# SwiGLU on one core: four rows per partition stored as one 64 KiB piece, the second pair multiplied in quarters

## The chip, the core and the metric

The kernel runs on one core of a Trainium2 chip. VectorE (DVE) multiplies, ScalarE (ACT) applies the activation, and 16 DMA engines move data between the device's memory (HBM) and the core's 128-partition on-chip memory (SBUF). DMAs are issued from three places, each with its own queue on all 16 engines: SyncE (SP, queue q1 in the profile), ACT (q10) and GpSimd (POOL, q0). The time is device microseconds for one launch; lower is better. The time before is the median of three runs.

## The reference

```python
x = np.random.randn(8192, 8192).astype(np.float32)

def reference(x):
    a, b = np.split(x, 2, axis=-1)
    silu_b = b / (1 + np.exp(-b))
    return a * silu_b
```

Each row of 8192 float32 holds 4096 values of `a`, then 4096 of `b`; the output row is 4096 wide. The input is 268.4 MB and the output 134.2 MB, and each byte is moved once.

## The kernel before

**Tiling.** Two neighbouring rows belong to one partition, so a tile is 128 partitions x 2 rows: 64 KiB of input per partition (8 MiB in all), one contiguous block of HBM, and 32 KiB of output per partition (4 MiB), contiguous too. There are 32 tiles. Three slots of 64 KiB per partition (`slots`, L39) hold them in turn; tile `i` uses slot `i % 3`.

**One tile.** `load(i)` (L54, the DMA at L55) is issued from SP. `swiglu(i)` (L67) writes silu(b) over b on ACT (`gate`, L72) and then a times that on DVE (`prod`, L76), into the front 32 KiB of the same slot. `store(i)` (L81, the DMA at L85) sends that front to HBM. A page line with L72 is thus a gate, L76 a product, L55 a load and L85 a store.

**Order.** The order is written out by hand. Each engine runs its own instructions in program order, and an instruction waits for what `follows_from_others` (L44) leaves in place: a gate for its load, a product for its gate, a store for its product, and the load of tile `i + 3` for the store of tile `i`, whose slot it takes. SP issues the loads in order, so a load that waits holds back every later one. Once a DMA is issued its packets stand in that issuer's queue on the 16 DMA engines.

**Queues.** Stores go out from ACT, except for five of the odd tiles in the second half (17 to 25), which go out from POOL (L83), and the last tiles', which go out from SP.

**Head and tail.** Tile 0 is gated and multiplied one row at a time and its store split in three (512 KB, 1536 KB, 2048 KB), so that the second half of its slot can be reloaded early (L94 to L99, `free`); tiles 1 and 2 are done one row at a time with one store. The last tile is loaded in two halves (L115, L116); its second row is gated, and multiplied, in two pieces of 2048 columns, and each row is stored by itself (L118 to L121).

Of the kernel before, what the change touches and what calls it, by code (L numbers as in the profile page):

```python
# [1 line left out]

# [4 lines left out]

_SILU = mybir.ActivationFunctionType.Silu


@with_exitstack
def kernel(
    ctx: ExitStack,
    tc: tile.TileContext,
    x: bass.AP,
    out: bass.AP,
):

    nc = tc.nc
    N, M = x.shape
    half = M // 2
    P = nc.NUM_PARTITIONS
    R = 2
    BUFS = 3  # L30

    xv = x.tensor.reshape([N // R, R * M]).ap()
    ov = out.tensor.reshape([N // R, R * half]).ap()
    ntiles = N // (P * R)
    last = ntiles - 1

    pool = ctx.enter_context(tc.tile_pool(name="sbuf", bufs=1))
    ctx.enter_context(tc.manual_schedule())
    slots = [pool.tile([P, R * M], x.dtype, name=f"slot{s}") for s in range(BUFS)]  # L39
    loads, gates, prods, stores = ([[] for _ in range(ntiles)] for _ in range(4))  # L40

    newest = {}

    def follows_from_others(inst, i, current, earlier):  # L44


        targets = [t for kind in current for t in kind[i]]
        targets += [t for kind in earlier for j in range(i % BUFS, i, BUFS) for t in kind[j]]
        for t in targets:
            if t is not newest.get(inst.ins.engine):  # L50
                tc.declare_no_dep(inst.ins, t.ins, reason="ordered by the other waits")
        newest[inst.ins.engine] = inst

    def load(i, c0=0, cw=R * M, free=None):  # L54
        inst = nc.sync.dma_start(  # L55
            out=slots[i % BUFS][:, c0 : c0 + cw], in_=xv[i * P : (i + 1) * P, c0 : c0 + cw]
        )
        if free:
            for t in loads[i - BUFS] + gates[i - BUFS] + prods[i - BUFS] + stores[i - BUFS]:
                if t is not free and t is not newest.get(inst.ins.engine):  # L60
                    tc.declare_no_dep(inst.ins, t.ins, reason="ordered by the other waits")
            newest[inst.ins.engine] = inst
        else:
            follows_from_others(inst, i, [], [loads, gates, prods])
        loads[i].append(inst)

    def swiglu(i, k0=0, k1=R, c0=0, cw=half, gated=None):  # L67
        rows = slots[i % BUFS].rearrange("p (k s c) -> p k s c", k=R, s=2)
        a = rows[:, k0:k1, 0, c0 : c0 + cw]
        b = rows[:, k0:k1, 1, c0 : c0 + cw]  # L70
        o = slots[i % BUFS][:, : R * half].rearrange("p (k c) -> p k c", k=R)
        gate = nc.scalar.activation(out=b, in_=b, func=_SILU)  # L72
        follows_from_others(gate, i, [], [loads, gates, prods, stores])
        if gated:
            gated()
        prod = nc.vector.tensor_mul(out=o[:, k0:k1, c0 : c0 + cw], in0=a, in1=b)  # L76
        follows_from_others(prod, i, [loads], [loads, gates, prods, stores])
        gates[i].append(gate)
        prods[i].append(prod)

    def store(i, c0=0, cw=R * half):  # L81
        eng = nc.scalar if i < last - 1 else nc.sync
        if i % 2 and ntiles // 2 <= i < ntiles // 2 + 10:  # L83
            eng = nc.gpsimd
        inst = eng.dma_start(  # L85
            out=ov[i * P : (i + 1) * P, c0 : c0 + cw], in_=slots[i % BUFS][:, c0 : c0 + cw]
        )
        follows_from_others(inst, i, [loads, gates], [loads, gates, prods, stores])
        stores[i].append(inst)

    for i in range(BUFS):
        load(i)
    for i in range(last):
        if i == 0:  # L94

            swiglu(i, 0, 1)
            swiglu(i, 1, 2, gated=lambda: [store(0, 0, half // 4), store(0, half // 4, half * 3 // 4)])
            load(BUFS, M, M, free=prods[0][-1])
            store(i, half, half)  # L99
        elif i < BUFS:  # L100
            for k in range(R):
                swiglu(i, k, k + 1)
            store(i)
        else:
            swiglu(i)
            if i == last - 1:
                swiglu(last, 0, 1)
            store(i)
        nxt = i + BUFS
        if nxt == BUFS:  # L110
            load(nxt, 0, M)
        elif nxt < last:
            load(nxt)
        elif nxt == last:
            load(last, 0, M)  # L115
            load(last, M, M)  # L116

    store(last, 0, half)  # L118
    for c0 in range(0, half, half // 2):
        swiglu(last, 1, 2, c0, half // 2)  # L120
    store(last, half, half)  # L121


# [1 line left out]
_INS = ['x']  # L125
_OUTS = [((8192, 4096), 'float32')]


# [23 lines left out]
```

## Time and profile before

| | us |
|---|---|
| median of three runs | 935.2 (935.12 to 935.31) |
| the profiled execution's span | 934.1 |
| DVE busy | 278.9 |
| ACT busy | 226.8 |
| DVE, one product of a pair of rows, 128 x 8192 (28 of them) | 8.69 |
| ACT, one gate of a pair of rows, 128 x 8192 (28 of them) | 7.03 |
| DVE, one product of 128 x 4096 (7) | 4.43 |
| ACT, one gate of 128 x 4096 (7) | 3.61 |
| store of 4 MiB from ACT, from issue to landing, median of 24 | 34.7 |
| ACT waiting for loads, in total | 690.0 |

The span runs from the first to the last instruction of the profiled execution; the runs are timed without it, and lie 1.1 us above it. "Busy" is the sum of an engine's own instructions. In the page's second part each digit is the busy share of one fortieth of the span, in tenths. In the table of DMA queues the share is the time that the queue's packets took, out of 16 engines' span. The chain of waits follows the work that ended last back to the start. Idle time of an engine that doesn't bound the kernel costs nothing.

### The profile page before, as it was taken

The numbers are of one execution on the slowest core, as the hardware profiler recorded it, in microseconds if no ns is written. First come the engines' busy times: TensorE is split into PE (matmuls) and PEld (weight loads), VectorE is DVE, ScalarE is ACT, GpSimd is POOL, SyncE is SP. The second block draws the span as 40 slices with busy tenths as digits, with TensorE's granted clock in tenths as the row PEclk, the third lists the DMA queues.
The fourth block names the chain that finished last, engine by engine and source line by source line (L and its number), as shares of the span: only waits on it lengthen the run. The fifth ranks groups of instructions, "written<-read, shape, count | busy, mean of one in ns | idle before, by whom it ended". The sixth has DMA issues, their size and how long they took to land.

```text
span 934.1 us, 228 instructions
## 1 busy us (share of the span) xinstructions
DVE 278.9 (30%) x37; ACT 226.8 (24%) x38; POOL 3.0 (0%) x9
## 2 busy tenths in 40 slices
DVE  0333123332133321333312333133331233312342
ACT  0431320233302333113331133311333113331141
POOL 0000000000000000000000000000000000000000
DMA  9999999999999999999999999999999999999998
GB/s 404 418 425 435 429 450 424 446 429 425 448 420 436 427 450 425 425 439 452 432 415 455 413 443 428 431 445 427 431 428 459 415 428 445 429 445 428 428 427 383
DMA packets 9937, 402.67 MB, mean 431 GB/s; under 512 B 1104, under 2 KB 1104, under 8 KB 1232
## 3 DMA queue, kind: packets, MB, share of 16 engines
q1 hardware_dynamic: 5328, 276.83, 68.6%
q10 hardware_dynamic: 3888, 104.86, 26.0%
q0 software_dynamic: 720, 20.97, 5.2%
q14 instruction: 1, 0.01, 0.0%
HBM read 268.44 MB, written 134.22 MB: 431 GB/s over the span
## 4 chain that ended last, share of the span: by engine, by line
DMA 74%; DVE 10%; ACT 7%; issue 6%; another core or an unknown queue 1%; DVEq 0%; SPq 0%; POOL 0%; ACTq 0%; POOLq 0%
DMA slot<-in_x_dram 40%; DMA out_dram<-slot 34%; DVE slot L76 10%; ACT slot L72 7%; DVEq L147 0%; SPq L55 0%; POOL out_dram L85 0%; ACTq L85 0%; DVEq L76 0%; POOLq L147 0%
## 5 line engine op out<-in xcount | busy, mean ns | idle before, releaser
L76 DVE TENSOR_TENSOR slot<-slot 128x8192 f32<-128x8192 f32 (+2 forms) x37 | 278.9, 7539 | 641.4 <-ACT slot L72 641.1
L72 ACT ACTIVATE slot<-slot 128x8192 f32<-128x8192 f32 (+2 forms) x37 | 225.5, 6105 | 690.0 <-DMA slot<-in_x_dram 690.0
L85 POOL DMA_DIRECT2D out_dram<-slot x5 | 2.8, 558 | 756.8 <-DVE slot L76 756.8
L72 ACT ACT_TABLE_LOAD x1 | 1.3, 1283 | 0.7 <-PEq L136 0.7
L136 POOL MEMSET const-bfloat16-1.0<- 128x1 bf16 x1 | 0.1, 102 | 0.0
L136 POOL MEMSET const-float32-0.0<- 128x1 f32 x1 | 0.1, 98 | 0.2 <-issue 0.2
L136 POOL MEMSET const-float32-1.0<- 128x1 f32 x1 | 0.1, 98 | 0.0
L136 POOL MEMSET const-uint8-127<- 128x1 uint8 x1 | 0.1, 98 | 0.0
## 6 DMA issues: line engine op xcount, KB each, us to landing
out_dram<-slot ACTq DMA_DIRECT2D x24, 4096.0 KB, 34.7
out_dram<-slot POOLq DMA_DIRECT2D x5, 4096.0 KB, 33.8
slot<-in_x_dram SPq DMA_DIRECT2D x4, 4096.0 KB, 29.7
out_dram<-slot SPq DMA_DIRECT2D x1, 4096.0 KB, 19.3
out_dram<-slot SPq DMA_DIRECT2D x2, 2048.0 KB, 14.5
out_dram<-slot ACTq DMA_DIRECT2D x1, 2048.0 KB, 47.0
out_dram<-slot ACTq DMA_DIRECT2D x1, 1536.0 KB, 41.8
out_dram<-slot ACTq DMA_DIRECT2D x1, 512.0 KB, 24.6
```

The costliest lines, as they stand in the source:

```text
L72: gate = nc.scalar.activation(out=b, in_=b, func=_SILU)
L76: prod = nc.vector.tensor_mul(out=o[:, k0:k1, c0 : c0 + cw], in0=a, in1=b)
L85: inst = eng.dma_start(out=ov[i * P : (i + 1) * P, c0 : c0 + cw], in_=slots[i % BUFS][:, c0 : c0 + cw])
L136: nc = _bacc.Bacc("TRN2", target_bir_lowering=False, num_devices=1)
```

## The change

Tiles become groups of four neighbouring rows per partition. There are 15 groups, and the last four rows of each partition's share (tiles 30 and 31 of before) are still done as two pairs.

The three slots keep their size but have roles. `even` and `odd` are used by the groups in turn; `side` by every group. A group's first pair of rows is loaded into its own slot (`acc`), its second pair into `side`. Each load takes 64 KiB per partition, and in HBM the pieces of neighbouring partitions now begin 128 KiB apart (view `x4`). The first pair is gated and multiplied whole, in place, into the front half of `acc`. The second pair is gated and multiplied in four quarters (`quarters`: one row, 2048 columns each) out of `side` into the back half of `acc`. Then `acc` holds 64 KiB of output per partition and is stored whole (8 MiB) from ACT.

`side` is reloaded for the next group when the four quarter products are done. `acc` is reloaded for the group after the next when its store has landed. Both loads are issued from SP, in that order, so the next group's side load stands ahead of the wait for the store. The first three loads are issued at once: the first pair of group 0, its second pair, the first pair of group 1.

The head of before (tile 0's split store and early reload) and POOL's five stores are gone. At the end tile 30 is done whole in one of the two slots; tile 31 is loaded into `side` in two halves, one per row, its second row's gate and product in two pieces of 2048 columns, and the stores of tile 30 and of each row of tile 31 go out from SP. `ordered` keeps, of all the waits, those on the instructions named and on the newest one of the same engine.

The added lines, with the lines between them that stay; the functions above are removed:

```diff
+    W = 2 * M
+    ntiles = N // (2 * P)
+    ngroups = ntiles // 2 - 1
...
+    x4 = x.tensor.reshape([N // 4, 4 * M]).ap()
+    o4 = out.tensor.reshape([N // 4, 4 * half]).ap()
+    x2 = x.tensor.reshape([N // 2, W]).ap()
+    o2 = out.tensor.reshape([N // 2, M]).ap()
     pool = ctx.enter_context(tc.tile_pool(name="sbuf", bufs=1))
     ctx.enter_context(tc.manual_schedule())
...
+    even = pool.tile([P, W], x.dtype, name="even")
+    side = pool.tile([P, W], x.dtype, name="side")
+    odd = pool.tile([P, W], x.dtype, name="odd")
     newest = {}
...
+    def ordered(inst, needs):
+        ins = inst.ins
+        keep = [t.ins for t in needs]
+        if ins.engine in newest:
+            keep.append(newest[ins.engine])
+        tc.declare_no_dep(ins, group="all", keep=keep, reason="ordered by the waits that are kept")
+        tc.add_to_no_dep_group("all", ins)
+        newest[ins.engine] = ins
+        return inst
+    def load(slot, view, r, c, needs, c0=0, cw=W):
+        return ordered(
+            nc.sync.dma_start(
+                out=slot[:, c0 : c0 + cw], in_=view[r * P : (r + 1) * P, c + c0 : c + c0 + cw]
+            ),
+            needs,
+        )
...
+    def store(eng, view, r, c, slot, cw, prods):
+        return ordered(
+            eng.dma_start(out=view[r * P : (r + 1) * P, c : c + cw], in_=slot[:, c : c + cw]), prods
+        )
...
+    def swiglu(src, dst, d0, parts, landed):
+        s3 = src.rearrange("p (k s c) -> p k s c", k=2, s=2)
+        d3 = dst[:, d0 : d0 + M].rearrange("p (k c) -> p k c", k=2)
+        prods = []
+        for k0, k1, c0, cw in parts:
+            a = s3[:, k0:k1, 0, c0 : c0 + cw]
+            b = s3[:, k0:k1, 1, c0 : c0 + cw]
+            o = d3[:, k0:k1, c0 : c0 + cw]
+            gate = ordered(nc.scalar.activation(out=b, in_=b, func=_SILU), [landed])
+            prods.append(ordered(nc.vector.tensor_mul(out=o, in0=a, in1=b), [gate]))
+        return prods
+
+    whole = [(0, 2, 0, half)]
+    halves = [(1, 2, c, half // 2) for c in (0, half // 2)]
+    quarters = [(k, k + 1, c, half // 2) for k in range(2) for c in (0, half // 2)]
+
+    slots = [even, odd]
+    main = [load(even, x4, 0, 0, [])]
+    extra = load(side, x4, 0, W, [])
+    main.append(load(odd, x4, 1, 0, []))
+    for g in range(ngroups):
+        acc = slots[g % 2]
+        swiglu(acc, acc, 0, whole, main[g])
+        prods = swiglu(side, acc, M, quarters, extra)
+        done = store(nc.scalar, o4, g, 0, acc, W, prods[-1:])
+        if g + 1 < ngroups:
+            extra = load(side, x4, g + 1, W, prods)
         else:
...
+            extra = load(side, x2, ntiles - 1, 0, prods, 0, M)
+            final = load(side, x2, ntiles - 1, 0, prods, M, M)
+        if g + 2 < ngroups:
+            main.append(load(acc, x4, g + 2, 0, [done]))
+        elif g + 2 == ngroups:
+            main.append(load(acc, x2, ntiles - 2, 0, [done]))
...
+    acc = slots[ngroups % 2]
+    prods = swiglu(acc, acc, 0, whole, main[ngroups])
+    store(nc.sync, o2, ntiles - 2, 0, acc, M, prods)
+    prods = swiglu(side, side, 0, [(0, 1, 0, half)], extra)
+    store(nc.sync, o2, ntiles - 1, 0, side, half, prods)
+    prods = swiglu(side, side, 0, halves, final)
+    store(nc.sync, o2, ntiles - 1, half, side, half, prods)
```

More of the change, by code (lines that the diff above doesn't have):

```diff
@@ L28 @@
     P = nc.NUM_PARTITIONS
[L29 to L35, printed above, removed]
+    W = 2 * M
[5 more added lines that the diff above has]
+    o2 = out.tensor.reshape([N // 2, M]).ap()
     pool = ctx.enter_context(tc.tile_pool(name="sbuf", bufs=1))
@@ L38 @@
     ctx.enter_context(tc.manual_schedule())
-    slots = [pool.tile([P, R * M], x.dtype, name=f"slot{s}") for s in range(BUFS)]
-    loads, gates, prods, stores = ([[] for _ in range(ntiles)] for _ in range(4))
+    even = pool.tile([P, W], x.dtype, name="even")
+    side = pool.tile([P, W], x.dtype, name="side")
+    odd = pool.tile([P, W], x.dtype, name="odd")
     newest = {}
[L44 to L52, printed above, removed]
@@ L54, in load @@
-    def load(i, c0=0, cw=R * M, free=None):
-        inst = nc.sync.dma_start(
-            out=slots[i % BUFS][:, c0 : c0 + cw], in_=xv[i * P : (i + 1) * P, c0 : c0 + cw]
-        )
[L58 to L62, printed above, removed]
-        else:
-            follows_from_others(inst, i, [], [loads, gates, prods])
-        loads[i].append(inst)
@@ L67, in swiglu @@
[L67 to L121, printed above, removed]
+    def ordered(inst, needs):
[7 more added lines that the diff above has]
+        return inst
```

## The prediction

> **What bounds the kernel now.** I read the page first: which resource is full.
>
> ```profile
> span 934.1 us, 228 instructions
> DVE 278.9 (30%) x37; ACT 226.8 (24%) x38; POOL 3.0 (0%) x9
> DMA  9999999999999999999999999999999999999998
> DMA packets 9937, 402.67 MB, mean 431 GB/s; under 512 B 1104, under 2 KB 1104, under 8 KB 1232
> q1 hardware_dynamic: 5328, 276.83, 68.6%
> q10 hardware_dynamic: 3888, 104.86, 26.0%
> q0 software_dynamic: 720, 20.97, 5.2%
> ```
>
> No compute engine is over 30%. The shares of SP's queue (q1), ACT's (q10) and POOL's (q0) add up to 99.8% of 16 DMA engines over the span. In the packet records the first packet starts 1.74 us into the span and the last ends at 932.87, 1.2 us before its end. So there is almost no idle DMA time to win back.
>
> Then stretches of the steady state (columns: DVE, ACT and POOL busy, clock, DMA share, GB/s), and the queues in four tiles of it:
>
> ```profile
> 150.00:300.00 150.00, 43.47 (x5) 35.15 (x5) 0.00 (x0) 1.00 1.00 434
> 526.00:790.00 264.00, 78.28 (x10) 63.26 (x9) 2.79 (x5) 1.00 1.00 435
> 930.00:934.10 4.10, 0.00 (x0) 0.00 (x0) 0.00 (x0) 1.00 0.36 152
> ```
>
> ```profile
> DMA packets 1152, 50.33 MB, mean 434 GB/s; under 512 B 128, under 2 KB 128, under 8 KB 128
> q1 hardware_dynamic: 576, 33.55, 66.7%
> q10 hardware_dynamic: 576, 16.78, 33.5%
> ```
>
> The second block is 300 to 416 us: 116.0 us for four tiles, 29.0 us a tile, with both queues at 100% together. With POOL's stores (526 to 790) the rate is the same 435. Packets of the two queues stand 576 to 576 though those of q1 are 64 KiB and those of q10 32 KiB: engines with work from both queues take one packet from each in turn. I use that below.
>
> Last the chain of waits, one lap of it, the durations by form, and the queue that waits:
>
> ```profile
> 212.94 36.47 DMA slot<-in_x_dram
> ...
> 249.43 7.04 ACT slot L72
> ...
> 256.49 8.70 DVE slot L76
> ...
> 265.21 34.70 DMA out_dram<-slot
> ```
>
> ```profile
> L76 DVE TENSOR_TENSOR slot<-slot 128x2048 f32<-128x2048 f32 x2 | 4.5, 2288 | 3.6 <-ACT slot L72 3.6
> L72 ACT ACTIVATE slot<-slot 128x2048 f32<-128x2048 f32 x2 | 3.7, 1902 | 6.1 <-DMA slot<-in_x_dram 6.1
> SPq L55 <- DMA out_dram<-slot: 832.6, 30, 37.3
> ```
>
> One slot's lap is 36.5 + 7.0 + 8.7 + 34.7 = 87 us, three tiles of 29.0; with three slots a load and a store are always in flight. The chain names ACT and DVE, but their 15.7 us lie beside other slots' transfers. SP's 832.6 us of waiting are only its sequencer; its ring holds packets nearly all that time.
>
> **The change, part by part.** The bytes are the same, so the question is what each packet costs and whether the engines ever run dry.
>
> *Packets, saved.* Before, an engine handles 552 data packets and 69 completion packets (34 loads, 35 stores). After: 31 loads of 8 MiB with 8 packets each, two of 4 MiB and 15 + 3 stores, also 8 each: 51 x 8 = 408 data packets and 51 completions. 144 data packets go, because a 64 KiB store piece goes as one packet where two 32 KiB pieces did. That a stored piece goes whole is what loads show, whose 64 KiB are one packet now. The records last 2418 ns for 64 KiB and 1213 ns for 32 KiB, so two small ones cost 8 ns more; they overlap by some 4 ns, and from starts (1209.5 ns for 32 KiB; 29.00 us less 8 of these and two completions leaves 2414 for 64 KiB) the difference is 4.7 ns. 144 x 4.7 = 0.68 us, at most 144 x 8 = 1.15. The 18 completions at 5 to 9 ns each add 0.09 to 0.16. Saving 0.8 us, bounds 0.7 to 1.3. I take the spacing, since it is what fills the time.
>
> The Trainium skill's page "DMA: Bandwidth & Descriptors", section "Anatomy of one DMA", gives a transfer a fixed cost of about 2 us; by that rule alone 18 fewer transfers would be worth 36 us. The trace speaks against counting it: shares of 1.00 over 150 us show transfers following one another without a gap.
>
> *Instructions, added and free.* Gates: 16 whole at 7.03 + 60 quarters at 1.90 + 7.4 at the end = 234 us (226.8 before). Products: 16 x 8.69 + 60 x 2.29 + 9.0 = 285. Both are far below 934 and hidden by transfers. What matters is the time from a side landing to the group's last product: 1.90 + 4 x 2.29 + handovers of some 0.1 = 11.2 us, against 15.8 for a whole pair (7.04 + 8.70).
>
> *The new order, walked through.* 8 MiB alone take 2/3 of 29.0 = 19.3 us. T is the end of a group's fourth quarter product. At T ACT issues the 8 MiB store and SP the next side load; SP then stops in order at the load that waits for that whole store. Left in SP's ring at T is part of the next group's first pair, whose load ran alone during the 11.2 us (plus 1.5 for landing and issue): 19.3 - 12.7 = 6.6 us of work. It shares with the store one to one (now both 64 KiB) and lands at T+13. Side load and store share then; the store's last 12.7 us take 25.4: it lands at T+38.6. The side load has 6.6 left and lands at T+45.2. The freed slot's load is issued at T+39, behind it, and runs on alone for 12.7 us until T+57.9, the next T. The lap closes at 57.9 us, 24 packets of 2.414, with no gap. Two covers carry it: 6.6 us of side load after the store has landed, and 6.6 us of the first pair's load at T. Queued behind SP's wait is only the next group's side load, which could not start earlier. Behind ACT's wait for the product is the next group's first gate, whose data lands 13 us later.
>
> What the covers must hold: landing spreads of 16 engines (1.4 to 2.7 us between first and last completion packet), 0.5 us to the waiting engine, and issue to first packet: 1.0 us on idle engines (0.74 to 1.74), 3.5 us behind others' packets (82.5 to 86.06). The spread does not add fully, since an engine that is early in one is early in the next; 0.5 + 3.5 = 4.0 is under 6.6. Beyond that, each us costs 15 us over the kernel. I take 0, upper end below under the rivals.
>
> *Head and tail.* The first side lands where the second load does now (ACT starts on it at 42.6), T is 53.8, and the third load (ACT starts on it at 66.0) still flows: no gap. Dropped with the old head are small stores; around 60 us its packets ran late (+0.55 us on each of 16 loads in step, +0.75 in sum over 37 to 63). Worth 0 to -0.75; I take 0, as the new head starts its first store in a similar way. The tail: the last T is 53.8 + 14 x 57.9 = 864; the last half lands near 910, and its gate and products need 1.9 + 4.6 us plus issue, while 4 MiB + 2 MiB of ready stores (9.7 + 4.8 us) flow. No gap. Today the last products too hide behind stores. The end spread, 1.4 us, may move by up to 0.7 either way.
>
> *POOL's queue, removed.* Its cover is the same 435 GB/s with and without it: 0, at most 0.2 saved.
>
> *Load pitch, changed.* Each load reads 64 KiB per partition at 128 KiB steps instead of 64. No row shows that pitch. Below: nothing gained, since loads alone already run at the packet time of 2418. Above: the nearest row is that late round at 60 us, 0.55 us per round; once in each of 15 groups it is 8.3 us. I take 0, as 64 KiB in one piece is the same packet and steady packets with power-of-two steps show no lateness today.
>
> The Trainium skill's same page, "Latency and other measured facts", speaks against the change here: copies with a row pitch of 512 KiB ran at 207 GB/s where 214 is full, and worse at larger pitches. Taking that whole 3.3% as an estimate for two thirds of 930 us would be +20 us. It tells of a four times larger pitch; no run here shows either.
>
> *Sum.* Profiled span 934.1 - 0.8 = 933.3. The median of the runs shown, 935.2, is 1.1 above the span: 935.2 - 0.8 = **934.4 us**.
>
> **Rivals.**
>
> F, faster: the 0.75 us of the old head go too and the end spread gives 0.7: 934.4 - 1.45 = 932.9. For: both are in the trace. Against: the new head has a first store of its own, and 16 engines that take packets in turn still end apart. 10%.
>
> S1, slower: the doubled pitch makes a round of load packets late once per group, at L55's successors: +8.3, 942.7. For: lateness hits in step, all 16 engines at once, and all packets being equal keeps them in step. Against: steady packets are at 2418 to the nanosecond. It decides from 0.18 us per group (2.7 us). 12%.
>
> S2, slower: SP's in-order wait for an 8 MiB store. If engines favoured loads two to one, the side load would land before the store, and the wait's 1.5 us of landing and issue would be bare in each lap: 15 x 1.5 = 22, 957. It decides when store landing plus issue come over 6.6 us later than in the walk. Against: 576 to 576. Partial forms, a us or less bare per lap, would end near 940 to 950. 10%.
>
> N, the packets don't merge: stores go on in 32 KiB packets, only 18 completions saved: 935.1. 6%.
>
> **How the numbers follow.** The forecast has 62%, at 933.6 to 935.6 by itself (saving 0.7 to 1.3, spread). About 0.2%, 1.9 us, is what can be told from no change: under 933.3 is faster, over 937.1 slower. Forecast and N give nearly all of same, 0.67 with a little to either side; F and a sliver of the forecast 0.11; S1 and S2 0.22. F to the upper edge of the forecast hold 0.78; mild forms of S1 and S2 up to 940 bring it over 0.8. Range 932.7 to 940.
>
> **What would show it.** Right: about 7345 packets (459 x 16), DMA shares still summing to 99.8%, gates of main pairs every 57.9 us, stores landing 39 us after issue, side loads 45, main loads 32. Wrong: a slice with a DMA digit under 9 or a lap over 58.1 us (S2, with ACT and SP both waiting); 64 KiB packets lasting over 2418 ns, so shares over 100% with fewer GB/s (S1); near 9,000 packets (N). A prediction on the wrong side of 937 would mean one of the two 6.6 us covers is not there.

## The result, and the profile after

| | before | after |
|---|---|---|
| median of the runs, us | 935.25 (935.12 to 935.31) | 957.17 (956.03 to 958.81) |
| ratio, 95% interval | | 1.0234 (1.0222 to 1.0246) |
| span of the profiled execution, us | 934.1 | 955.4 |

The kernel is 22 us slower. The forecast was no change, 934.4, and its range ended at 940. Runs that took over 1.5% longer than the fastest run of the same kernel are left out of the times and ratios in this document. First the page of the changed kernel: the span, DVE's work, the DMA digits, the packets, and the queues with their shares.

```profile
span 955.4 us, 287 instructions
DVE 281.4 (29%) x79; ACT 230.7 (24%) x80; POOL 0.2 (0%) x4
DMA  9999999999999999999999999999999999999998
DMA packets 7346, 402.67 MB, mean 421 GB/s; under 512 B 816, under 2 KB 816, under 8 KB 816
q1 hardware_dynamic: 5184, 276.83, 68.9%
q10 hardware_dynamic: 2160, 125.83, 30.4%
```

The edit does what it says: 9937 packets have become 7346, the bytes are the same, and no compute engine is busier than 29%. Yet the DMA row still reads 9 in every slice but the last, as before, and the shares still add up to 99.3%. By this view the engines are as full as before, and they move 421 GB/s instead of 431. Stretches of the steady state (columns: DVE, ACT and POOL busy, clock, DMA share, GB/s) say the same more sharply:

```profile
150.00:300.00 150.00, 44.07 (x14) 35.98 (x14) 0.00 (x0) 1.00 1.00 419
300.00:900.00 600.00, 175.88 (x50) 143.38 (x50) 0.00 (x0) 1.00 1.00 424
```

Before, 150 to 300 us moved 434 GB/s at a share of 1.00; now it is 419 at a share of 1.00. A "busy" DMA engine is one with a packet in hand, and a packet can be in hand for longer. So the loss sits inside packets and not in gaps between them. Single laps, from one group's last product to the next group's, show that it comes and goes:

```profile
231.00:291.59 60.59, 17.59 (x5) 14.34 (x5) 0.00 (x0) 1.00 1.00 419
...
529.68:588.18 58.50, 17.59 (x5) 14.34 (x5) 0.00 (x0) 1.00 1.00 430
588.18:646.47 58.29, 17.59 (x5) 14.34 (x5) 0.00 (x0) 1.00 1.00 432
646.47:706.76 60.29, 17.59 (x5) 14.34 (x5) 0.00 (x0) 1.00 1.00 422
```

The same work takes 58.3 us in one lap and 60.6 in another. The chain of waits (start, length, what) gives a lap's parts:

```profile
291.59 48.56 DMA side<-in_x_dram
340.17 1.92 ACT side L72
342.12 8.91 DVE odd L73 x4
351.04 48.83 DMA side<-in_x_dram
```

The quarters take the 11 us that were reckoned (1.92 + 8.91 and handovers), and the rest is the side load: issued at 291.59, landed 48.6 us later where the walk said 45.2. Over all laps the mean is 59.54 us instead of 57.9. What stands around it, in the timeline (start, length, engine, line, operation) and in the table of DMA issues (last column: us from issue to landing):

```profile
291.59 0.33 SPq L53 DMA_DIRECT2D side<-in_x_dram  x1
291.59 0.36 ACTq L61 DMA_DIRECT2D out_dram<-even  x1
306.37 7.03 ACT L72 ACTIVATE odd<-odd 128x8192 f32<-128x8192 f32 x1 [18.34 <-DMA odd<-in_x_dram]
...
336.21 0.33 SPq L53 DMA_DIRECT2D even<-in_x_dram  x1
```

```profile
side<-in_x_dram SPq DMA_DIRECT2D x15, 48.6
even<-in_x_dram SPq DMA_DIRECT2D x8, 29.8
odd<-in_x_dram SPq DMA_DIRECT2D x8, 30.4
out_dram<-even ACTq DMA_DIRECT2D x8, 44.3
out_dram<-odd ACTq DMA_DIRECT2D x7, 43.8
```

The store lands 44 us after T, the end of the group's last product (the walk: 38.6), so the freed slot's load is issued at T+44.6, and the side load, the only other work in SP's ring, lands at T+48.6. SP's own waits (total, times, longest) confirm whom it waits for, once per lap:

```profile
SPq L53 <- DMA out_dram<-even: 306.6, 7, 44.3
SPq L53 <- DMA out_dram<-odd: 306.3, 7, 44.5
```

**Where the 21 us are.** No single view answers this, so I sorted the packet records of the trace by engine (a packet belongs to the engine on which another ended as it began; the engine numbers below are only labels) and summed, per engine, what each 64 KiB packet takes above 2418 ns and each 32 KiB packet above 1213 ns. Three names are used from here on. A **turn** is the first store packet that an engine takes after at least three load packets in a row; its price is the excess of the two load packets just ahead of it. A **cold start** is a load whose first packet follows on an engine whose loads had run out. **T** is the end of a group's last product, when the 8 MiB store is issued.

| us per engine | before | after |
|---|---|---|
| 15 turns, 956 ns each | 0.0 | 14.3 |
| stretched packets at cold starts | 0.0 | 2.8 |
| other stretched packets | 1.5 | 2.4 |
| engine without a packet | 0.0 | 2.5 |
| packets and completions saved | | -0.75 |
| last engine's end behind the mean engine's | 1.1 | 2.5 |

The differences add up to 21.2 us, against 21.3 between the spans. Two engines at the turn after T = 291.59 (start in us; L load, S store; +ns above 2418), and engine 0 at T = 112.34, where the turn cost nothing:

```
T=291.59  engine 0:  288.0 L | 290.4 L+6 | 292.9 L+166 | 295.4 L+1148 | 299.0 S
T=291.59  engine 6:  288.1 L | 290.5 L | 292.9 L+1393 | 296.7 S | 299.1 L
T=112.34  engine 0:  110.0 L | 112.4 L | 114.8 L | 117.2 S | 119.6 L
```

Two things are to be seen. The first store packet comes 4.9 to 7.4 us after T: the engine first handles the one or two load packets that begin after T. And in the first two rows the load packets around T take 1.3 and 1.4 us longer, together.

### The profile page after: what moved, and what is told of

It reads as the page before. It is cut to its first block, busy times and chain, and to the rows that moved or that the text cites. A ratio compares the mean times of both kernels' runs of the same rounds, so it can differ in the third digit from the quotient of the medians.

```text
span 955.4 us, 287 instructions
## 1 busy us (share of the span) xinstructions
DVE 281.4 (29%) x79; ACT 230.7 (24%) x80; POOL 0.2 (0%) x4
## 2 busy tenths in 40 slices
DMA packets 7346, 402.67 MB, mean 421 GB/s; under 512 B 816, under 2 KB 816, under 8 KB 816
## 4 chain that ended last, share of the span: by engine, by line
DMA 78%; DVE 13%; ACT 4%; another core or an unknown queue 3%; DVEq 0%; issue 0%; SPq 0%
DMA side<-in_x_dram 70%; DVE even L73 7%; DVE odd L73 7%; DMA out_dram<-odd 5%; DMA odd<-in_x_dram 3%; ACT side L72 3%; ACT odd L72 1%; DVE side L73 0%; DVEq L131 0%; SPq L53 0%
## 5 line engine op out<-in xcount | busy, mean ns | idle before, releaser
L72 ACT ACTIVATE side<-side 128x2048 f32<-128x2048 f32 (+1 forms) x63 | 117.0, 1924 | 409.2 <-DMA side<-in_x_dram 409.2
L73 DVE TENSOR_TENSOR even<-even 128x8192 f32<-128x8192 f32 x8 | 69.5, 8692 | 182.6 <-ACT even L72 182.6
L73 DVE TENSOR_TENSOR odd<-odd 128x8192 f32<-128x8192 f32 x8 | 69.5, 8692 | 177.6 <-ACT odd L72 177.6
L73 DVE TENSOR_TENSOR even<-side 128x2048 f32<-128x2048 f32 x32 | 71.2, 2286 | 145.5 <-ACT side L72 145.5
L73 DVE TENSOR_TENSOR odd<-side 128x2048 f32<-128x2048 f32 x28 | 62.3, 2285 | 138.8 <-ACT side L72 138.8
L72 ACT ACTIVATE odd<-odd 128x8192 f32<-128x8192 f32 x8 | 56.2, 7029 | 149.4 <-DMA odd<-in_x_dram 149.4
L72 ACT ACTIVATE even<-even 128x8192 f32<-128x8192 f32 x8 | 56.2, 7029 | 148.8 <-DMA even<-in_x_dram 148.8
L73 DVE TENSOR_TENSOR side<-side 128x2048 f32<-128x2048 f32 (+1 forms) x3 | 8.9, 3000 | 15.6 <-ACT side L72 15.6
## 6 DMA issues: line engine op xcount, KB each, us to landing
out_dram<-side SPq DMA_DIRECT2D x2, 2048.0 KB, 14.5
side<-in_x_dram SPq DMA_DIRECT2D x15, 48.6
```

Of the source, the lines that this page charges most:

```text
L72: gate = ordered(nc.scalar.activation(out=b, in_=b, func=_SILU), [landed])
L73: prods.append(ordered(nc.vector.tensor_mul(out=o, in0=a, in1=b), [gate]))
```

## The experiments

The expectations name these theories. **PITCH**: reading 64 KiB pieces 128 KiB apart slows the loads (S1 of the prediction). **LATE**: SP's in-order wait for the whole store issues the freed slot's load too late (S2's place). **START**: a store that begins among loads costs each engine about 1 us, whatever went before. **DRY** (later **RESTART**): it costs that only when the loads had run out and begun again since the last store. **SIZE**: the 64 KiB store pieces do it. **RING**: a load ring that isn't kept deep does it. **SAME INSTANT**: the store and the side load are issued within 10 ns, and that does it. A few expectations name others (**FRESH**, **DELAY**, **TURN**) and say there what they mean.

**Is it the pitch?** In the first run the changed kernel reads contiguous pieces (the rows go to other places of the output); in the second the kernel before reads at 128 KiB steps and stores at 64 KiB steps.

```diff
-            extra = load(side, x4, g + 1, W, prods)
+            extra = load(side, x2, 2 * g + 3, 0, prods)
-            main.append(load(acc, x4, g + 2, 0, [done]))
+            main.append(load(acc, x2, 2 * g + 4, 0, [done]))
```

> The changed kernel with its schedule, sizes and waits kept, but each load reads one contiguous 8 MiB block of HBM (64 KiB per partition at steps of 64 KiB, as before the change) instead of 64 KiB pieces at steps of 128 KiB. The rows of the output are then permuted. Theory PITCH (load packets last longer because of the doubled step): the packets above 2418 ns go, and the time falls to 935 to 940. Theory START (each lap the store queue starts from empty beside loads that run alone, and the start costs) and theory LATE (the freed slot's load is issued too late behind the wait for the 8 MiB store): no difference, 955 to 959, load packets stretched as much as now (19.6 us per engine over the kernel).

```diff
-  in_=xv[i * P : (i + 1) * P, c0 : c0 + cw]
+  in_=x4[i // 2 * P : (i // 2 + 1) * P, i % 2 * R * M + c0 : i % 2 * R * M + c0 + cw]
```

> The kernel before, with only its addresses changed: loads read 64 KiB per partition at steps of 128 KiB and stores write 32 KiB per partition at steps of 64 KiB, as a group of four rows has them. Theory PITCH: slower, by two thirds of the loss or more, 948 to 957, with load packets above 2418 ns in the steady state. Theories START and LATE: 934 to 937, no such packets between 100 and 900 us.

With the pitch undone: 953.72 us (944.09 to 957.89), 1.0181 (1.0117 to 1.0245), turns of 999 ns and 20.0 us of stretch; most of the loss stays, though one of the four runs took 944. With the pitch alone: 935.29, 1.0001 (0.9992 to 1.0011). Neither window moves toward the other kernel; the first is of the changed kernel with contiguous reads, the second of the kernel before with the doubled pitch:

```profile
300.00:900.00 600.00, 175.88 (x50) 143.38 (x50) 0.00 (x0) 1.00 1.00 422
```

```profile
300.00:900.00 600.00, 179.09 (x21) 147.61 (x21) 2.79 (x5) 1.00 1.00 433
```

PITCH falls. The Trainium skill's page "DMA: Bandwidth & Descriptors", section "Latency and other measured facts", from which the prediction made an estimate of +20 us, speaks of pitches from 512 KiB on; at 128 KiB these runs show nothing of it. The profile's sign that the prediction had set for S1, full shares with fewer GB/s, did appear: it told of long packets, and the pitch was only one way to them.

**Is it the wait for the whole store?** Two ways to have the freed slot sooner. In the first, the first pair's half goes out as soon as it is multiplied. In the second, each half has its own store, and the slot is reloaded in two halves, each behind its own store; the first half's store went out when the side load had landed, 10.8 us ahead of T (334.92 against 345.73 in the trace), and not the 3 us that were expected. In both the second half's store still starts at T.

```diff
+        early = store(nc.scalar, o4, g, 0, acc, M, first)
-        done = store(nc.scalar, o4, g, 0, acc, W, prods[-1:])
+        done = store(nc.scalar, o4, g, M, acc, M, prods[-1:])
-            main.append(load(acc, x4, g + 2, 0, [done]))
+            main.append(load(acc, x4, g + 2, 0, [early, done]))
```

> The changed kernel, but a group's first pair is stored (4 MiB, 32 KiB per partition) as soon as it is multiplied, some 28 us before the second pair's 4 MiB. The store queue then always holds work, and the freed slot's load waits for only 4 MiB after the last product. Theories START and LATE: the loss goes, 934.5 to 938, lap 58.0. Theory PITCH: most of the loss stays, 948 to 957.

```diff
+        done = [store(nc.scalar, o4, g, c, acc, M, p) for c, p in ((0, first), (M, prods[-1:]))]
+            main.append([load(acc, x4, g + 2, 0, [done[j]], j * M, M) for j in range(2)])
```

> The changed kernel with two 4 MiB stores issued together near the end of the group (the first after the last quarter gate, some 3 us before the last product) and the freed slot reloaded in two halves, each waiting for its own store: the store queue still starts from empty beside loads that run alone, but the first half of the slot's load no longer waits for 8 MiB. Theory LATE: the loss goes, 935 to 938. Theory START: only the late part goes, 15 laps still pay about 1 us of stretched load packets each at the start of the stores, 946 to 951. Theory PITCH: 948 to 957, and stretched packets not tied to the start of the stores.

Both are within 2.1 us of before: 937.15 (936.76 to 937.49), 1.0018 (1.0008 to 1.0027), and 937.32 (936.82 to 939.0), 1.0025 (1.0014 to 1.0036). The second's window, SP's waits and chain:

```profile
300.00:900.00 600.00, 176.47 (x51) 150.41 (x51) 0.00 (x0) 1.00 1.00 434
```

```profile
SPq L53 <- DMA out_dram<-even: 264.2, 14, 28.0
SPq L53 <- DMA out_dram<-odd: 253.2, 14, 25.0
```

```profile
287.70 47.13 DMA side<-in_x_dram
334.86 1.92 ACT side L72
336.80 8.91 DVE odd L73 x4
345.72 47.14 DMA side<-in_x_dram
```

SP's longest wait for a store is 28 us instead of 44, the lap is 58.02 us (345.72 less 287.70), and the rate is the 434 GB/s of before. The first of the two has 2 turns per engine. The second keeps all 15, now at the first half's store, and pays 81 ns for each on the mean: the first, at the head, took 908, the second 282, and the others 24 or less. So a turn isn't dear by itself, against START, and LATE has the place right. Both kernels also have smaller pieces and earlier stores, so they don't yet say what made the turn dear.

**The other direction: later still.** The second pair in one piece again, which moves T back by 4.6 us:

```diff
-        prods = swiglu(side, acc, M, quarters, extra)
+        prods = swiglu(side, acc, M, whole, extra)
```

> The changed kernel with the second pair's gate and product whole instead of in quarters, so the last product comes 4.6 us later after the side load's landing. By the prediction's walk 6.6 us of the first pair's load are left at the last product and hide this: no difference, 955 to 960. If a new store's first packet comes only after the two packets that each engine has already taken (5 to 8 us after the issue in the trace), that cover is used up already, and each lap grows by most of the 4.6 us: 990 to 1030, with idle engines ahead of the store.

1052.08 us (1049.57 to 1055.63), 1.1251 (1.1226 to 1.1276), beyond even the upper range of the expectation. Its window:

```profile
300.00:900.00 600.00, 156.46 (x18) 126.52 (x18) 0.00 (x0) 1.00 0.95 379
```

Here the share does fall, to 0.95: an engine is without a packet for 51 us in all, 3.4 per lap. Another 70 us are stretch. Of a delay of 4.6 us per lap, 15 x 4.6 = 69 us, the kernel made 95 us more. The quarters are worth that much to this order; it has no slack at T at all.

**Is it the size of the pieces?** The change's store as two column halves of 32 KiB, both after the last product, and the reload waiting for both:

```diff
-        done = store(nc.scalar, o4, g, 0, acc, W, prods[-1:])
+        done = [store(nc.scalar, o4, g, M, acc, M, prods[-1:]), store(nc.scalar, o4, g, 0, acc, M, first)]
```

> The changed kernel with its 8 MiB store cut into two DMAs of 32 KiB pieces, both issued after the last product, and the freed slot's load waiting for both. Order and waits stay. Theory SIZE: stretched packets fall from 19.6 us per engine to under 4. Theory RING: they stay at 14 or more. In either case the engines, which take a packet from each queue in turn, now favour loads two to one, so theory LATE expects the store to land after the side load and the freed slot's load to find the engines idle: 1.5 us or more of idle time per lap, by the walk of the prediction with sharing two to one, 950 to 985 in all. Without LATE: 936 to 942.

985.8 us (982.66 to 987.2), 1.0544 (1.0527 to 1.0562):

```profile
300.00:900.00 600.00, 169.65 (x48) 140.67 (x49) 0.00 (x0) 1.00 0.97 410
```

The stretch stays (21.6 us, turns of 775 ns), and 27 us of empty engines, 1.8 per lap, come on top. With 32 KiB pieces against 64 KiB loads the store takes twice as many alternations. In the lap from T = 353.66 its slot's load is issued at 407.94, so T+54.3 and not T+44.6, when the side load's gate has already begun (404.33). The loads run out once per lap, and the packet records of one engine show both prices, the cold start and the turn (T = 353.66):

```
341-344: S S S S, then nothing | 347.5 L+836 | 350.7 L | 353.1 L+37 | 355.6 L+727 | 358.7 S
```

This is S2's bare wait, with S2's two-to-one ratio. SIZE falls as the cause of the dear turn; the 64 KiB piece even saves the change from worse.

**A stream with nothing but the turn.** To separate the store's start from the wait, I wrote a stream: 31 loads of 8 MiB alternate between `even` and `odd`, `side` is loaded once, and each time an even load lands, `side` is stored whole from ACT as one of 16 groups of the output. No gate of the reference and no product is computed. The loads never wait for a store.

```python
needs = loads[i - 2 : i - 1] if i > 1 else []
needs = needs + reads[(i - 2) // 2 : (i - 2) // 2 + 1] if i > 1 and i % 2 == 0 else needs
loads.append(load(slots[i % 2], x2, i, 0, needs))
if i % 2 == 0:
    gate = nc.scalar.activation(out=few, in_=slots[0][:, 0:1], func=_SILU)
    reads.append(ordered(gate, [loads[i]]))
    store(nc.scalar, o4, i // 2, 0, side, W, SIDE)
```

> No computation worth the name and no dependence of stores on loads: 31 loads of 8 MiB alternate between two slots, so that SP's ring always holds one whole load behind the running one, and after every second load ACT starts one 8 MiB store of 64 KiB pieces from a third slot, from an empty queue; the output is that slot's content. Bytes, packet sizes and the mix are those of the changed kernel. Theory START (turning from loads alone to loads and stores costs about 1 us per engine each time, however full the load ring is): 15 us of stretched load packets, one group at each store's start, 948 to 952. Theory DRY (the turn costs only where the load ring is down to its last packets while the new store and the new load are on their way): no stretched packets after the head, 933 to 937.

> The stream of loads and stores of the run before with its 8 MiB stores cut into two DMAs of 32 KiB pieces, both issued where the one was. Theory SIZE (engines stretch load packets where 64 KiB store packets stand beside them, at the turn above all, and do not where they are 32 KiB): stretched time falls from 6.2 us per engine to under 2, at the same bytes. Theory RING (stretching follows from how the rings fill, not from the size of the store's pieces): 4 to 8 us, as with 64 KiB.

947.23 us with 64 KiB pieces and 953.24 with the same store as two DMAs of 32 KiB pieces. The time of the first is nearly START's, but for another reason: the last store stands alone, with 8.3 us of empty engines at the end. Its 16 turns cost 87 ns each (the first 821), so START falls a second time, and SIZE too, since the smaller pieces have more stretch (8.2 us against 6.2), not less.

**Does it matter how late the store is, or how deep the ring?** The stream with the store put off by six spare activations (11.4 us) after the even load's landing. In the first run below the next even load is issued at the landing, so the ring stays deep; in the second it too waits for the delay, and the store and the load are issued about 2 us apart, with a ring as shallow as the change has.

```diff
+            for _ in range(6):
+                burns.append(ordered(nc.scalar.activation(out=burn, in_=side[:, 0:2048], func=_SILU), SIDE + burns[-1:]))
```

> The stream of loads and 8 MiB stores of 64 KiB pieces, with 6 activations of 128 x 2048 (11.4 us) on ACT between an even load's landing and the store; the next load is issued at the landing, as before. At the store's issue SP's ring holds the rest of the running load (3 packets or so per engine) and the 8 packets of the next. Theory RING (the turn from loads alone to loads and stores costs an engine about 1 us where its load ring is down to its last packets, with the next load issued only together with the store): turns as cheap as in the stream without the delay (87 ns per engine and turn). Theory DELAY (the cost comes with where in a load the store starts, or with compute before it): about 900 ns per turn.

```diff
-            reads.append(ordered(gate, [loads[i]]))
+            ordered(gate, [loads[i]])
...
+            gate = nc.scalar.activation(out=few, in_=slots[0][:, 1:2], func=_SILU)
+            reads.append(ordered(gate, [loads[i]]))
```

> The same stream, but the next load too is issued only after the 11.4 us of activations, together with the store, as in the changed kernel: the ring is down to the last packets of the running load when both arrive. No product, no data dependence and contiguous reads. Theory RING: about 950 ns of stretched load packets per engine and turn, as in the changed kernel. If the cost needs something else of the changed kernel (VectorE's products, or a store of fresh data): 90 to 300 ns.

The deep one took 971.52 us (964.59 and 978.44), the shallow one 955.23, of which the delay and the lone store at the end are part. Turns: 137 ns in the deep one, the first of them 1234; in the shallow one 86 ns, the first 1253 and the others 4. RING falls. The deep one's 25.6 us of other stretch in its late laps I can't explain.

**Is it the same instant?** In the trace after, both issues stand at 291.59. In the change, a one-column activation between the last product and the side load moves that load 0.6 us behind the store:

```diff
+        prods = prods + [ordered(nc.scalar.activation(out=few, in_=side[:, 0:1], func=_SILU), prods[-1:])]
```

> The changed kernel with one tiny activation (128 x 1) on ACT right behind the store's issue, for which the side load waits too: SP issues that load some 0.6 us after ACT issues the store, where both now follow the same product and are issued 5 ns apart. Theory SAME INSTANT (the two DMAs issued together, the store's issue lasting 362 ns against 338 alone, make the first store packets come late and the load packets ahead of them stretch): turns fall from 956 ns per engine to about 90, 13 us go, and with the store landing earlier some of the late freed slot's load too: 936 to 945. Theory FRESH (the cost belongs to storing data that was just multiplied, or to the order of the changed kernel otherwise): no difference, 955 to 959.

And in the shallow stream, a one-column product (into a column of the stored slot) releases both at once, 5 ns apart:

```diff
+            both = nc.vector.tensor_mul(out=side[:, W - 1 : W], in0=slots[0][:, 0:1], in1=burn[:, 0:1])
+            reads.append(ordered(both, burns[-1:] + sent[-1:]))
+            sent.append(store(nc.scalar, o4, i // 2, 0, side, W, reads[-1:]))
```

> The stream with the delay and the shallow load ring, but the store and the next load wait for the same tiny product on VectorE, so that both are issued at the same instant instead of 2 us apart; that product writes one column of the stored slot. Theory SAME INSTANT: turns rise from 86 ns per engine to 700 or more. Otherwise they stay at 80 to 300 ns.

Apart, the change still takes 953.1 us (951.16 to 958.4), 1.0196 (1.0171 to 1.0221), with turns of 893 ns. Together, the stream takes 1016.36 us, with turns of 511 ns and 51 us of stretch spread over the stretches where loads and stores alternate. The first says no. The second has its dear turns only from the sixth lap on: in the four laps from 113.67 to 290.51 both are issued at the same instant too, and the turns cost 18 ns on the mean. So the same instant isn't enough to make a turn dear. What stretches this stream's later laps I can't explain.

**Do the loads have to have run dry?** Sorting the turns of the change after each engine's first: on 105 of 224 the engine's loads had started cold since its last store. These cost 1243 ns on the mean, each over 300; the other 119 cost 695, half of them (48%) 300 or less. In the first stream, the shallow one and the second two-store kernel nearly no turn follows a cold start, except the kernel's first, and that one cost 0.8 to 1.4 us in every version of the change and every stream. So the shallow stream was changed in one thing: the odd load is issued only when the even one has landed, so that the loads run out once per lap and start again 9 us ahead of the store.

```diff
+        if i > 1 and i % 2:
+            needs = dry[-1:]
...
+            if i:
+                gate = nc.scalar.activation(out=few, in_=slots[1][:, 0:1], func=_SILU)
+                dry.append(ordered(gate, [loads[i - 1]]))
```

> The stream with the 11.4 us delay and the shallow ring (3 ns per turn after the first), but every odd load is issued only when the even one has landed, so that the load stream runs dry once a lap, 11 us before the turn. Theory RESTART: turns cost 700 to 1300 ns per engine. Theory TURN: under 100 ns, as without the restart.

The stream whose loads never run dry, and then the one that does (columns: ACT and POOL busy, clock, share, GB/s; then one start of it in the timeline):

```profile
300.00:700.00 400.00, 80.48 (x56) 0.00 (x0) 1.00 1.00 432
```

```profile
300.00:700.00 400.00, 71.58 (x56) 0.00 (x0) 1.00 0.96 401
347.00:354.00 7.00, 1.21 (x3) 0.00 (x0) 1.00 0.37 159
354.00:361.00 7.00, 6.87 (x5) 0.00 (x0) 1.00 1.12 451
361.00:368.00 7.00, 3.61 (x3) 0.00 (x0) 1.00 0.86 300
368.00:404.00 36.00, 0.00 (x0) 0.00 (x0) 1.00 1.01 437
```

```profile
353.22 0.33 SPq L53 DMA_DIRECT2D odd<-in_x_dram  x1
362.65 0.34 ACTq L61 DMA_DIRECT2D out_dram<-side  x1
```

```
never dry:  286.2 L | 288.7 L | 291.1 L+8 | 293.5 S | 295.9 S
run dry:    354.2 L+788 | 357.4 L | 359.8 L | 362.2 L+14 | 364.6 L+1011 | 368.1 S
```

The loads start at 353.22, run at full rate, and the store is issued at 362.65. From 361 to 368 the rate is 300 GB/s, and from 368 on it is 437 again. The 4 ns of the shallow stream's later turns have become 1209 ns on the 224 turns after a dry start, each over 680; the 16 turns of the last lap, which has no dry start, cost 0 (the remaining 16 are the engines' first). The time, 1010.58 us, contains the 50.6 us of empty engines that the edit brings. RESTART holds in the stream.

A dry start also brings the 16 engines into step: their first store packets begin within 0.5 to 1.1 us of one another in the stream that runs dry, and within 0.9 to 3.6 us in the one that doesn't. That is not what costs the change its time: there the first store packets of its dear laps are 1.9 to 3.9 us apart, and those of its cheap ones 1.3 to 3.4.

Sorted by lap, the change fits RESTART better than by engine. In three of its 14 laps after the first no engine started cold, and the turns cost 14, 266 and 44 ns on the mean, though the stores carry fresh data there too, against FRESH. In the other eleven the engines without a cold start of their own (71 turns) pay 1091 ns, nearly as much as those with one; only one of the eleven, with three cold engines, stays cheap for the rest (149 ns). The run with contiguous reads, the one with the side load 0.6 us behind and the two with spare activations below have nine laps without a cold start between them, at 0 to 106 ns; in their other laps the engines without one pay 717 to 948. This is a sorting and not an experiment.

**Taking the late load out of the change itself.** I tried to keep 8 MiB stores of 64 KiB pieces and have no dry start. First, the side slot reloaded in two halves, the first as soon as its row's two quarters are multiplied:

```diff
+            extra = [load(side, x4, g + 1, W, [prods[2 * k + 1]], k * M, M) for k in range(2)]
```

> The changed kernel, but the side slot is reloaded in two halves of 32 KiB per partition, the first as soon as its row's two quarters are multiplied, some 4.6 us before the last product. The store, its size and its start from empty, and the late load of the freed slot stay. Theory DRY: the load ring is refilled before it is down to its last packets, the stretched packets at the store's start go (14 us) and about 8 us of the loss stay, 941 to 946. Theory START: the stretched packets stay, 954 to 959. Theory LATE alone (all the loss is the freed slot's late load): 954 to 959 as well.

956.24 us (954.05 to 960.3), 1.0229 (1.0199 to 1.0258). One lap's store, the load of the freed slot, and the first gate behind the landing of the side load's second half:

```profile
286.64 0.36 ACTq L61 DMA_DIRECT2D out_dram<-even  x1
324.62 0.33 SPq L53 DMA_DIRECT2D even<-in_x_dram  x1
339.17 3.71 ACT L72 ACTIVATE side<-side 128x2048 f32<-128x2048 f32 x2 [5.99 <-DMA side<-in_x_dram]
```

The freed slot's load is issued at T+38.0, 14.5 us before the side load has landed, so here the late load is gone, which the expectation had staying. Turns fell to 364 ns and empty time to 1.3 us, as DRY had it; but 13.0 us of stretch came elsewhere, 8.3 of it on store packets, and the last engine's end moved to 5.3 us behind the mean one's, so the time is the one that START and LATE had. Nine of the 14 laps after the first have no cold start, and their turns still cost 270 ns on the mean, in one lap 857. So ending the late load doesn't by itself win the time back, and a dry start is not the only thing that stretches packets; what does it here stays open. Then the store and the reload of its slot as two DMAs of 64 partitions each, and both edits together:

```diff
+        for h in range(2):
+            rows = slice(g * P + h * P // 2, g * P + (h + 1) * P // 2)
+            inst = nc.scalar.dma_start(out=o4[rows, 0:W], in_=acc[h * P // 2 : (h + 1) * P // 2, 0:W])
+            done.append(ordered(inst, prods[-1:]))
```

> The changed kernel, but the 8 MiB store is issued as two DMAs of 64 partitions each, still 64 KiB pieces and both at the last product, and the freed slot is reloaded in two such halves, each waiting for its own store. The first half can be issued well before the side load has landed. Theory LATE alone: the loss goes, 934 to 938. Theories DRY and START with LATE: the late part (about 8 us) goes and the stretched packets at the store's start stay, 947 to 952.

> Both edits together: side reloaded in two column halves as they come free, store and freed slot's reload in two partition halves. Theories DRY with LATE: both parts of the loss go, 934 to 938, lap 58.0, and the packet saving of the 64 KiB pieces may show against before (935.4). Theory START with LATE: 947 to 952.

1382.02 us (1374.09 to 1390.57), 1.4806 (1.4758 to 1.4855), and 1404.95 (1401.08 and 1408.81), 1.5021 (1.4972 to 1.507). Both lose far more than the change, with other packets stretched (told at the end), and say nothing on the theories. Last, the side load held back behind the store by two spare activations (3.8 us) or four (7.6 us), to let the store's packets in earlier:

```diff
+        for _ in range(2):
+            wait = nc.scalar.activation(out=burn, in_=side[:, 0:2048], func=_SILU)
+            burns.append(ordered(wait, prods[-1:] + burns[-1:]))
+        prods = prods + burns[-1:]
```

> The same with two spare activations (3.8 us). Theory RESTART: the store lands one to two packets further ahead, most laps have no late load, 934 to 945. Theory TURN: 950 to 958.

> The changed kernel with four spare activations of 128 x 2048 (7.6 us) on ACT behind the store's issue, which the side load waits for: that load enters SP's ring some 8 us after the store, while the store's packets flow. The store then lands about two packets further ahead of the side load and the freed slot's load reaches the engines before they run dry. Theory RESTART (all the loss follows from the freed slot's late load: the load stream runs dry for a moment and starts cold, and the next turn to loads and stores then costs about 1 us): idle time, cold starts and dear turns all go but for the first turn, 934 to 938, lap 58.0. Theory TURN (dear turns belong to the changed order whatever ran before): 5 us or less go, 950 to 958.

953.58 us, 1.0188 (1.0171 to 1.0206), and 954.57, 1.0183 (1.0161 to 1.0206): a little faster than the change and far from before. RESTART's times (934 to 945, 934 to 938) are missed and TURN's (950 to 958) are met. But with four activations the store still landed at T+44.1 and the side load 4.5 us after it (in the lap from T = 288.81), as in the change, so the late load was still there and the runs can't tell the two apart. Sorted as above, their turns after a cold start cost 1251 and 1137 ns, the others 550 and 599.

No version of the change beats the kernel before. The nearest, with two 4 MiB stores, is 0.18% slower.

## Why the prediction was wrong

The predicted gain came; a loss came with it that the walk of the lap had put at nothing.

- **Packets and saving: right.** 7346 packets against some 7345, and 0.75 us per engine against 0.8. N falls: the stored pieces go as 64 KiB packets of 2418 ns. The fixed cost of about 2 us that the prediction names from the Trainium skill's page "DMA: Bandwidth & Descriptors", section "Anatomy of one DMA", and sets aside, is given there for transfers issued from GpSimd. Of the 18 transfers that went, 13 were ACT's and SP's, and the saving of 0.75 us shows nothing of it.
- **Quarters: right.** 11 us from the side's landing to T.
- **Head, tail and POOL's queue: about right.** At the end of the kernel the last engine stands 2.5 us behind the mean one instead of 1.1, twice the 0.7 allowed. F doesn't show.
- **The pitch (S1): rightly taken at 0.**
- **The walk: the step that failed** is "It shares with the store one to one ... it lands at T+38.6", and with it the cover of "6.6 us of side load after the store has landed". The ratio is nearly right: after two store packets in a row the two queues alternate one to one. What the walk left out is the store's two ends. It let the store's packets flow from T on, though the same text had read 3.5 us from issue to first packet off the trace of before, and used them only for the next load. Measured, a store's first packet comes 3.5 to 8.3 us after T, median 6.0 over engines and laps. Then 8 store and 7 load packets, 15 x 2.414 = 36.2 us, run before the store's completion packet, which so stands at T+42.3 on a median engine; the last engine's comes 0.8 to 2.3 us later, and the landing 0.3 to 0.5 after that: T+44.1 (42.8 to 44.9 over the first 14 laps), not T+38.6. The side load lands 3.2 to 6.4 us after the store, 4.5 on the mean, and not 6.6. On the engines the cover is thinner: when the freed slot's load is issued, a median engine has some 2.3 us of side load left.
- **What the covers must hold: 4.0 us, held against 6.6.** With 4.5 the sum would have said "just enough", and for the bare wait that is nearly so, though some engines run out in most laps: they stand empty for only 2.5 us of the kernel. S2 named the place, SP's in-order wait for the 8 MiB store, and its 957 is the measured time. But its ground, two loads to one store, is wrong for this kernel (it is what the 32 KiB version does, at 986), and so is its term, 1.5 us bare per lap: 2.5 of the 21 us are bare. That 957 was met is chance.
- **What no rival held:** after a wait that is *nearly* covered, loads run out on some engines and start cold, and in the laps where that happens the next turn to loads and stores costs each engine about a microsecond. The turns are 14.3 of the 21 us, with 2.8 more at the cold starts themselves. Since all packets stay in hand, no share falls and no digit changes.

Shown are: that smaller and earlier stores, which end the late load, bring the lap to 58.0 us; that in a stream a dry start alone turns 4 ns into 1209; that pitch, piece size and the depth of the ring are not the cause. Argued, not shown: that the dear turns of the change come from its dry starts. The sorting by lap speaks for it, and for the 71 dear turns whose own engine had no cold start being dear because others had one; the run with the side load in halves, without a late load and as slow as the change, says that it can't be the whole account. Argued too is that the mix of dry starts makes one execution differ from the next. Open is why loads that have started from empty give way so slowly to the next store, what stretches the packets of that run, and what the two unexplained streams do.

## What to carry to other kernels

When a transfer is issued into full DMA queues, let its packets begin one or two of the other queue's packets late, not at its issue, and carry that through every later landing; with 64 KiB packets it was 6 us. Leave a cover larger than that before an in-order queue's next issue, because running dry can cost more than the gap: in the stream the restart made the next mix of loads and stores 1.2 us slower on every engine, and in the change the dear turns came to 14.3 us beside 2.5 of empty engines. When shares are full and GB/s fall, compare packet durations, not gaps, and free a buffer in halves before making its store larger.

## What the runs showed of the hardware

- **A new queue's first packet comes late.** In the changed kernel 3.5 to 8.3 us from the issue of a store to its first packet with 64 KiB loads in flight, 1.0 us on idle engines. The Trainium skill's page "DMA: Bandwidth & Descriptors", section "Queues, rings and completion order", says that an engine goes round the queues that have work, one packet at a time. The records agree once both queues flow; they also show two load packets beginning (292.9 and 295.4 on engine 0) after the store's issue at 291.59 and before its first packet; the section has nothing on that.
- **A completion packet waits its turn too.** On engine 0 the store's last 64 KiB packet ends at 332.81, a load packet follows to 335.22, and only then comes the 9 ns packet that completes the store: 2.4 us more.
- **A store that begins after a dry start** stretches the last one or two load packets by 1.2 us per engine on the mean in both the change (1243 ns, on engines with a cold start) and the stream (1209); the first 4 or 8 MiB store after the kernel's start pays 0.8 to 1.4.
- **Transfers over 64 partitions.** In the first kernel with them, 64 KiB load packets took 3.9 us on the mean, up to 8.5, and not 2.42. One 116 us window of it, in which four tiles moved before (the traced execution took 1429 us):

```profile
DMA packets 523, 28.31 MB, mean 244 GB/s; under 512 B 91, under 2 KB 91, under 8 KB 91
q1 hardware_dynamic: 361, 19.92, 80.8%
q10 hardware_dynamic: 162, 8.39, 18.8%
```

  The shares are full at 244 GB/s. The same page's section "Rules for kernel authors" advises against two transfers to halves of the partitions because they serialize; here they cost 48%.
- **ACT's issue of the store** lasts 362 ns when SP issues 5 ns earlier and 338 when it issues 0.6 us later; the time didn't follow it.
